# Column tiles: all high weight halves and then all low ones, and a fifth score product of 128 rows

## The chip, the cores and the metric

The kernel runs on one core of a Trainium2 chip. The metric is device time in microseconds (us). The engines are TensorE (PE; its weight loads are listed apart as PEld), VectorE (DVE), ScalarE (ACT), GpSimd (POOL) and SyncE (SP), which here issues the loads.

## The reference

One encoder layer on 256 tokens of width 2048, all in float32:

```
h = RMSNorm(x);  z = h @ w_in  -> q-latent 512 | kv-latent 512 | rotary key 64 | conv 3 x 1024 | memory query 1024 | gates 3 x 2048
A: latent attention, 8 heads, scores = q_nope . k_nope (128 dims) + q_rope . k_rope (64 dims, key shared by the heads)
B: conv_B * dwconv3(conv_C * conv_v)          C: attention of 4 heads into 256 memory tokens
x = x + (sum_i sigmoid(gate_i) * (branch_i @ w_i)) @ w_o
u = dwconv3(RMSNorm(x) @ w_up);  x = x + (silu(a) * b) @ w_down;  out = RMSNorm(x)
```

## The kernel before

Activations stand feature-major, 128 features on the partitions and 256 tokens (T) along the free axis. To keep float32 accuracy each operand is split into two float32r halves: `hi`, a rounded copy that ACT makes (L138 for weights, L195 and L198 for activations), and `lo`, the rest, by a subtraction on DVE (L139, L196 and L199). A split activation chunk is one tile of 512 columns, [hi | lo], 256 each.

Weights come in blocks of 128 x 2048 (1 MB) from the SP queue into three `raw` buffers, and are split into three `hi` and two `lo` buffers. A column tile is 128 output features by 256 tokens. `mm` computes one through `acc`: for each row chunk k the high weights multiply the whole chunk of 512 columns (L165, giving hi.hi in the first PSUM half and hi.lo in the second), then the low weights multiply its high half of 256 columns (L166, lo.hi, summed into the first half). For the last chunk the order is reversed (L162, L163), so that the last matmul closes both halves. `total` adds the two halves (L186 on ACT, L188 on DVE). A tile has 16 row chunks on `h` (the normed inputs of both sub-layers) and on `mg` (the merged branches), 8 on `oa`, `yc` and `om` (the branches' outputs), and 22 on `f` (the feed-forward's inner columns), which come in two blocks of 11, each a call of `acc` of its own.

Elsewhere other helpers do the same: `acc1` (L174 to L176) sums hi.hi, lo.hi and hi.lo into one PSUM half, with 256 columns a matmul; `values` (L371 to L373) has tokens on the partitions and 512 weight columns moving; L521 multiplies the rotary key's weights, halves side by side, by 512 columns.

The stages in order: latents; memory keys and values; rotary key; memory queries and heads; gated convolution with the latent projections and heads in between; gates, branch projections and merge into `mg` (L649 to L653); output projection (L662 on); feed-forward; and the last 512 output columns with tokens on the partitions. Each engine runs its own instructions in order. A planner sets that order ahead of time, by its own simulated time line; so pieces of one job can stand between the matmuls of another.

A head of latent attention (`latent_head`, then `attend`, L437) sums five products into the scores, for each half of the queries: three of split `q_nope` and `k_nope`, then two of the rotary part. A rotary query tile `e` has, for its head, the 64 rows of the high half and the 64 rows of the low half on the two halves of the partitions (which is above which goes by the head's parity); the rotary key `krs` stands there twice, [hi | lo] along the free axis. The fourth product takes all 128 rows of `e` with the key's high half; the fifth takes only the 64 rows of `e`'s high half, with the key's low half.

Of the kernel before, what the change touches and what calls it, by code (L numbers as in the profile page):

```python
# [19 lines left out]
P = 128  # L20
D = 2048
T = 256
# [15 lines left out]

# Columns of the packed per-partition constants.
COLS = {}  # L40
# [10 lines left out]
def _parts(c, bits, n):  # L51
    """c as a sum of n floats of few bits each, so that small integers times them are exact."""
    out = []
    for _ in range(n - 1):
        m, e = math.frexp(c)
        part = math.ldexp(round(math.ldexp(m, bits)), e - bits)
        out.append(part)
        c -= part
    out.append(c)
    return [float(np.float32(x)) for x in out]  # L60
# [16 lines left out]
def tile_kernel(ctx: ExitStack, tc: tile.TileContext, a, out):  # L77
    nc = tc.nc
# [23 lines left out]

# [1 line left out]
    cols = const.tile([P, NCOLS], F32, name="cols")  # L104
# [17 lines left out]

# [1 line left out]
    def load(src, n=WB, pieces=1):  # L124
# [21 lines left out]

    # A column tile's result stands in two parts, [hi.hi + lo.hi | hi.lo], or is summed in place.
    def psum(pool=mmps, tag="mm"):
# [7 lines left out]
    def acc(ps, hi, lo, off, xs, first, final):  # L156
        n = len(xs)
        for k, x in enumerate(xs):
            s = slice(off + k * P, off + (k + 1) * P)
            start, stop = first and k == 0, final and k == n - 1  # L160
            if stop:
                nc.tensor.matmul(ps[:, 0:T], lo[:, s], x[:, 0:T], start=False, stop=False)  # L162
                nc.tensor.matmul(ps, hi[:, s], x, start=start, stop=True)  # L163
            else:
                nc.tensor.matmul(ps, hi[:, s], x, start=start, stop=False)  # L165
                nc.tensor.matmul(ps[:, 0:T], lo[:, s], x[:, 0:T], start=False, stop=False)  # L166

# [15 lines left out]
    def total(ps):  # L183
        """The two parts of a column tile's result, added."""
        hl = temp("hl")
        nc.scalar.activation(hl, ps[:, T:], AF.Copy)  # L186
        t = temp("t")
        nc.vector.tensor_tensor(t, ps[:, 0:T], hl, op=ALU.add)  # L188
        return t

    def split(dst, src, gain=None):
        """src (times a gain) as two float32r halves."""
        w = dst.shape[1] // 2
        if gain is None:
            nc.scalar.activation(dst[:, 0:w], src, AF.Copy)  # L195
            nc.vector.tensor_tensor(dst[:, w:], src, f32(dst[:, 0:w]), op=ALU.subtract)  # L196
        else:
            nc.scalar.activation(dst[:, 0:w], src, AF.Copy, scale=gain)  # L198
            nc.vector.scalar_tensor_tensor(  # L199
                dst[:, w:], src, gain, f32(dst[:, 0:w]), op0=ALU.mult, op1=ALU.subtract  # L200
            )
# [16 lines left out]
    def feature_sums(sq):  # L218
        """Sums over features, tokens on partitions: [128, 2]."""
        ps = atps.tile([P, 2 * T], F32, tag="at", name="psm")  # L220
        for h in range(2):
            nc.tensor.matmul(
                ps[:, h : h + 1], sq[:, h * P : (h + 1) * P], ones[:, 0:1], start=True, stop=True
            )
        return ps[:, 0:2]
# [11 lines left out]
    def spread(r, dst=None):  # L237
        """A factor per token, tokens on partitions, as a row on every partition."""
        ps = atps.tile([P, 2 * T], F32, tag="at", name="pss")
        for h in range(2):  # L240
            dg = tmp.tile([P, P], F32, tag="dg", name="dg")
            nc.vector.tensor_scalar(dg, ident, r[:, h : h + 1], None, op0=ALU.mult)
            nc.tensor.matmul(ps[:, h * P : (h + 1) * P], ones, dg, start=True, stop=True)
        if dst is None:
            return ps[:, 0:T]
        nc.scalar.activation(dst, ps[:, 0:T], AF.Copy)
        return dst

    class Tokens:
        """Feature chunks times the norm's gain, split; and the sums of squares."""  # L250

# [4 lines left out]
        def load(self, n):  # L256
            """The next n chunks, two of them in a tile."""
            i = len(self.raw)
# [17 lines left out]

    # The tensor engine's clock rises while it works, so it starts before the data is there.
    wake = psum(atps, "at")
    for i in range(WAKE):
        nc.tensor.matmul(wake[:, 0:P], ones, ident, start=True, stop=True)  # L280

# [1 line left out]
    tok = Tokens(a["xT"], "mix", "h")  # L283
# [51 lines left out]
    def latent_factor(sq, name, scale):  # L335
        """The token's own norm and the latent's, in one factor."""
        e = tiny.tile([P, 2], F32, tag=name + "e", name=name + "e")
# [7 lines left out]

# [1 line left out]
    kx = []  # L347
# [11 lines left out]
    def values(src, n, nblk, xs, name):  # L359
        """Token-major values, split: for each half of the tokens [hi, lo] of 512 columns."""  # L360
        ps = [psum() for _ in range(2)]
# [26 lines left out]

# [1 line left out]
    pos = half(slot("pos", I32), 0)  # L390
# [21 lines left out]
    def rope(x, w):  # L412
        """x holds halves of 32 partitions; rotated in place, w columns of T."""
        sw = slot("sw")
# [9 lines left out]

# [1 line left out]
    def products(q, k):  # L426
        """The products of split queries and keys, [dims, hi | lo]."""
        return [(q[:, 0:T], k[:, 0:T]), (q[:, T:], k[:, 0:T]), (q[:, 0:T], k[:, T:])]

    def attend(terms, row, vslices, name, res):  # L430
        """terms: queries and keys to multiply, [dims, 256]; row: a factor per key; vslices: the
        split values' [128 keys, 128 dims] by key half. Adds [dims, 256 queries] tiles, split,
        to res."""
        ps = atps.tile([P, 2 * T], F32, tag="at", name="pss")
# [46 lines left out]
    def latent_head(h):  # L481
        r = slice(64 * (h % 2), 64 * (h % 2) + 64)
        e = half(qr[h // 2], h % 2)
        c = slice((h % 4) * P, (h % 4 + 1) * P)
        return attend(
            products(qn[h], kn[h]) + [(e, krs[:, 0:T]), (e[r], krs[r, T:])], half(fb, 0),
            [[(vh[:, c], vl[:, c]) for vh, vl in vn[h // 4]]], f"oa{h}_", oa,
        )
# [13 lines left out]
    def advance(start=None):  # L502
        """A stage of each head under way, then the first of another."""
        for g in list(flying):
            if next(g, 0) == 0:
                flying.remove(g)
        if start is not None:
            next(start)
            flying.append(start)

    # The rotary key, twice over, on partitions 0-63 and 64-127: one column tile holds the
    # halves of its 64 columns, which the sum then brings together.
    raw = next(load(a["wkr"], KC * ROPE))
# [9 lines left out]

# [1 line left out]
    qx = []  # L525
# [16 lines left out]

# [1 line left out]
    def conv(x, dst, w, wi, wn):  # L544
        """Three taps along tokens; w: the name of the taps' columns."""
        nc.scalar.activation(dst, x, AF.Copy, scale=col(w, wn + wi))  # L546
# [40 lines left out]
    def rotary_queries():  # L587
        hi, lo = block(a["wuq"][2])
        for i in range(2):
# [4 lines left out]
            rope(q, 2)  # L594
            # For each head its two halves above each other; the keys stand there twice.
            lows = slot("ql", F32R)
# [33 lines left out]

# [1 line left out]
    mg = [slot(f"mg{i}", F32R) for i in range(KC)]  # L632
# [22 lines left out]

# [1 line left out]
    x2 = [slot(f"xr{i}") for i in range(KC // 2)]  # L657
# [13 lines left out]

# [1 line left out]
    rfb = []  # L673
# [42 lines left out]

    # ---- the last columns with tokens on partitions, so that one half of the tokens is done,
    # normed and stored while the other is still multiplied ----
    gains = slot("gains")
# [85 lines left out]
def _rows(w):  # L805
    """[K, N] in column tiles: [tile, partition, row chunk, 128]."""
    k, n = w.shape
# [3 lines left out]
def _blocks(w, per):  # L811
    """Column tiles, `per` of them in a block: [block, partition, per * rows]."""
    t = _rows(w)
# [4 lines left out]
def _wide(w, per):  # L818
    """[K, N] in pieces of `per` row chunks by 512 columns: [piece, partition, per * 512]."""
    k, n = w.shape  # L820
# [4 lines left out]
def _colmajor(v):  # L825
    """[n * 128] as a column per 128."""
    return np.asarray(v).reshape(-1, P).T
# [83 lines left out]
```

## Time and profile before

| | us |
|---|---|
| median of 3 runs | 1663.72 (1663.1 to 1663.75) |
| span of the profiled execution | 1660.7 |
| PE busy | 1649.4 |
| DVE busy | 1136.8 |
| ACT busy | 843.2 |

The profiled execution gives a span from the first to the last instruction; the runs' time has about 3 us beside it. Matmuls are pipelined, so their busy times overlap, and the distance from start to start is what one costs. A wait of an engine is put down to what ended it.

### The profile page before, as it was taken

The numbers are of one execution on the slowest core, as the hardware profiler recorded it, in microseconds if no ns is written. First come the engines' busy times: TensorE is split into PE (matmuls) and PEld (weight loads), VectorE is DVE, ScalarE is ACT, GpSimd is POOL, SyncE is SP. The second block draws the span as 40 slices with busy tenths as digits, with TensorE's granted clock in tenths as the row PEclk, the third lists the DMA queues.
The fourth block names the chain that finished last, engine by engine and source line by source line (L and its number), as shares of the span: only waits on it lengthen the run. The fifth ranks groups of instructions, "written<-read, shape, count | busy, mean of one in ns | idle before, by whom it ended". The sixth has DMA issues, their size and how long they took to land.

```text
span 1660.7 us, 23629 instructions
## 1 busy us (share of the span) xinstructions
PE 1649.4 (99%) x9626; PEld 1444.8 (87%) x9626; DVE 1136.8 (68%) x1535; ACT 843.2 (51%) x1118; POOL 11.7 (1%) x23
## 2 busy tenths in 40 slices
PE   9999999999999999999999999999999999999998
PEld 9998898888888888888888888888888888888886
DVE  8756787676666666666666777777555777777554
ACT  8644555544545445444454655555444555555552
POOL 0000010000000000000000000000000000000000
PEclk9999999999999999999999999999999999999999
DMA  9555455344555554555565555554556555554563
GB/s 327 208 181 179 170 172 184 142 163 152 180 194 184 181 197 181 183 198 178 190 222 197 185 196 178 186 194 156 178 187 210 192 192 178 191 190 154 187 211 114
DMA packets 52443, 308.97 MB, mean 186 GB/s; under 512 B 6000, under 2 KB 7536, under 8 KB 22256
## 3 DMA queue, kind: packets, MB, share of 16 engines
q1 hardware_dynamic: 50688, 305.82, 52.2%
q8 instruction: 76, 1.25, 0.3%
q10 hardware_dynamic: 1008, 1.12, 0.2%
q0 software_dynamic: 640, 0.52, 0.1%
q14 instruction: 31, 0.25, 0.0%
HBM read 304.17 MB, written 2.10 MB: 184 GB/s over the span
## 4 chain that ended last, share of the span: by engine, by line
PE 98%; DMA 1%; issue 0%; DVE 0%; ACT 0%; SPq 0%; POOLq 0%; POOL 0%; DVEq 0%
PE ps L165 52%; PE ps L166 26%; PE ps L163 4%; PE ps L174 2%; PE ps L175 2%; PE ps L176 2%; PE ps L162 2%; PE pss L437 1%; PE ps L372 1%; PE ps L373 1%; PE ps L371 1%; PE ps L736 0%; PE ps L738 0%; PE ps L737 0%; DMA raw<-in_wkv 0%
## 5 line engine op out<-in xcount | busy, mean ns | idle before, releaser
L139 DVE TENSOR_TENSOR lo<-raw,hi 128x2048 fp32r<-128x2048 f32 (+2 forms) x312 | 649.7, 2083 | 371.5 <-PE ps L162 286.1
L165 PE MATMUL ps<-h,hi 128*128 128x512 f32 x2520 | 898.4, 398 | 0.0
L166 PE MATMUL ps<-h,lo 128*128 128x256 f32 x2520 | 708.3, 281 | 0.0
L138 ACT ACTIVATE hi<-raw 128x2048 fp32r<-128x2048 f32 (+2 forms) x312 | 543.6, 1744 | 81.1 <-PE ps L165 37.1
L165 PEld LDWEIGHTS ps<-h,hi 128*128 128x128 f32 x2520 | 473.4, 188 | 107.7
L166 PEld LDWEIGHTS ps<-h,lo 128*128 128x128 f32 x2520 | 475.8, 189 | 8.1
L186 ACT ACTIVATE hl<-ps 128x256 f32<-128x256 f32 x253 | 97.1, 384 | 440.8 <-PE ps L163 439.4
L165 PE MATMUL ps<-f,hi 128*128 128x512 f32 x588 | 208.7, 398 | 0.0
L166 PE MATMUL ps<-f,lo 128*128 128x256 f32 x588 | 165.4, 281 | 0.1
L165 PEld LDWEIGHTS ps<-f,hi 128*128 128x128 f32 x588 | 110.5, 188 | 25.6
L166 PEld LDWEIGHTS ps<-f,lo 128*128 128x128 f32 x588 | 111.0, 189 | 1.8 <-DVE lo L139 0.4
L188 DVE TENSOR_TENSOR t<-ps,hl 128x256 f32<-128x256 f32 x253 | 105.8, 418 | 9.3 <-ACT hl L186 9.3
L165 PE MATMUL ps<-mg,hi 128*128 128x512 f32 x240 | 85.1, 397 | 0.0
L546 ACT ACTIVATE v<-u,taps 128x256 f32<-128x256 f32 x88 | 44.8, 510 | 70.1 <-DVE u L683 70.1
L547 DVE SCALAR_TENSOR_TENSOR v<-u,taps,v 128x255 f32<-128x255 f32 x88 | 42.5, 484 | 48.8 <-ACT v L546 48.8
L166 PE MATMUL ps<-mg,lo 128*128 128x256 f32 x240 | 67.2, 281 | 0.0
L163 PE MATMUL ps<-h,hi 128*128 128x512 f32 x168 | 67.2, 400 | 0.0
L165 PEld LDWEIGHTS ps<-mg,hi 128*128 128x128 f32 x240 | 45.0, 188 | 10.2
L162 PE MATMUL ps<-h,lo 128*128 128x256 f32 x168 | 47.4, 282 | 0.0
L166 PEld LDWEIGHTS ps<-mg,lo 128*128 128x128 f32 x240 | 45.3, 189 | 0.8
L195 ACT ACTIVATE f<-si 128x256 fp32r<-128x256 f32 x44 | 18.4, 417 | 52.6 <-DVE si L689 52.6
L550 DVE SCALAR_TENSOR_TENSOR v<-u,taps,v 128x255 f32<-128x255 f32 x88 | 42.5, 484 | 3.0
(259 smaller groups left out, 1845.4 us busy)
## 6 DMA issues: line engine op xcount, KB each, us to landing
raw<-in_wup SPq DMA_DIRECT2D x88, 1024.0 KB, 4.8
raw<-in_win SPq DMA_DIRECT2D x83, 1024.0 KB, 4.8
raw<-in_wdn SPq DMA_DIRECT2D x56, 704.0 KB, 4.1
raw<-in_wo SPq DMA_DIRECT2D x16, 1024.0 KB, 4.8
raw<-in_wmk SPq DMA_DIRECT2D x8, 1024.0 KB, 4.9
raw<-in_wmv SPq DMA_DIRECT2D x8, 1024.0 KB, 4.8
raw<-in_woa SPq DMA_DIRECT2D x8, 1024.0 KB, 4.8
raw<-in_woc SPq DMA_DIRECT2D x8, 1024.0 KB, 4.7
```

Of the source, the lines that this page charges most:

```text
L138: nc.scalar.activation(hi[:, s], raw[:, s], AF.Copy)
L139: nc.vector.tensor_tensor(lo[:, s], raw[:, s], f32(hi[:, s]), op=ALU.subtract)
L162: nc.tensor.matmul(ps[:, 0:T], lo[:, s], x[:, 0:T], start=False, stop=False)
L163: nc.tensor.matmul(ps, hi[:, s], x, start=start, stop=True)
L165: nc.tensor.matmul(ps, hi[:, s], x, start=start, stop=False)
L166: nc.tensor.matmul(ps[:, 0:T], lo[:, s], x[:, 0:T], start=False, stop=False)
L174: nc.tensor.matmul(p1, hi[:, s], x[:, 0:T], start=start, stop=False)
L186: nc.scalar.activation(hl, ps[:, T:], AF.Copy)
L188: nc.vector.tensor_tensor(t, ps[:, 0:T], hl, op=ALU.add)
L546: nc.scalar.activation(dst, x, AF.Copy, scale=col(w, wn + wi))
L547: nc.vector.scalar_tensor_tensor(dst[:, 1:T], x[:, 0 : T - 1], col(w, wi), dst[:, 1:T], op0=ALU.mult, op1=ALU.add)
L550: nc.vector.scalar_tensor_tensor(dst[:, 0 : T - 1], x[:, 1:T], col(w, 2 * wn + wi), dst[:, 0 : T - 1], op0=ALU.mult, op1=ALU.add,)
```

## The change

`acc` no longer alternates. A call first issues the high matmuls of its row chunks, then all its low ones; where the call closes the tile, the high matmul of the last chunk is kept back and comes last. For the two blocks of `down` the first call issues 11 highs and 11 lows, the second 10 highs, 11 lows and one high. `latent_head` gives the fifth product all 128 rows of `e` and of the key's low half; this adds the product of the two low halves to the scores. The rest of the diff takes away comments and docstrings.

```
     def acc(ps, hi, lo, off, xs, first, final):
         n = len(xs)
-        for k, x in enumerate(xs):
-            s = slice(off + k * P, off + (k + 1) * P)
-            start, stop = first and k == 0, final and k == n - 1
-            if stop:
-                nc.tensor.matmul(ps[:, 0:T], lo[:, s], x[:, 0:T], start=False, stop=False)
-                nc.tensor.matmul(ps, hi[:, s], x, start=start, stop=True)
-            else:
-                nc.tensor.matmul(ps, hi[:, s], x, start=start, stop=False)
-                nc.tensor.matmul(ps[:, 0:T], lo[:, s], x[:, 0:T], start=False, stop=False)
+        ks = [slice(off + k * P, off + (k + 1) * P) for k in range(n)]
+        whole = n - 1 if final else n
+        for k in range(whole):
+            nc.tensor.matmul(ps, hi[:, ks[k]], xs[k], start=first and k == 0, stop=False)
+        for k in range(n):
+            nc.tensor.matmul(ps[:, 0:T], lo[:, ks[k]], xs[k][:, 0:T], start=False, stop=False)
+        for k in range(whole, n):
+            nc.tensor.matmul(ps, hi[:, ks[k]], xs[k], start=False, stop=True)
...
     def latent_head(h):
-        r = slice(64 * (h % 2), 64 * (h % 2) + 64)
         e = half(qr[h // 2], h % 2)
...
-            products(qn[h], kn[h]) + [(e, krs[:, 0:T]), (e[r], krs[r, T:])], half(fb, 0),
+            products(qn[h], kn[h]) + [(e, krs[:, 0:T]), (e, krs[:, T:])], half(fb, 0),
```

## Rows read from the trace of the kernel before

**Rows 1.** The page's busy times by engine, and the core's span and granted clock.

```profile
PE 1649.4 (99%) x9626; PEld 1444.8 (87%) x9626; DVE 1136.8 (68%) x1535; ACT 843.2 (51%) x1118; POOL 11.7 (1%) x23
...
core 0: 1660.7 us, clock 0.998
```

**Rows 2.** Waits of PE: line, waited for, us in total, times, longest.

```profile
PE pso L755 <- DVE dg L753: 2.7, 1, 2.7
PE ps L280 <- POOL ident masks.py:199: 1.5, 1, 1.5
PE ps L174 <- ACT h L198: 1.1, 1, 1.1
```

**Rows 3.** The chain that ended last, share of the span by line.

```profile
PE ps L165 52%; PE ps L166 26%; PE ps L163 4%; PE ps L174 2%; PE ps L175 2%; PE ps L176 2%; PE ps L162 2%; PE pss L437 1%; PE ps L372 1%; PE ps L373 1%; PE ps L371 1%; PE ps L736 0%; PE ps L738 0%; PE ps L737 0%; DMA raw<-in_wkv 0%
```

**Rows 4.** PE groups: line, names, shapes, count | busy us, mean ns | idle before.

```profile
L165 PE MATMUL ps<-h,hi 128*128 128x512 f32 x2520 | 898.4, 398 | 0.0
...
L165 PE MATMUL ps<-f,hi 128*128 128x512 f32 x588 | 208.7, 398 | 0.0
...
L165 PE MATMUL ps<-mg,hi 128*128 128x512 f32 x240 | 85.1, 397 | 0.0
...
L165 PE MATMUL ps<-yc,hi 128*128 128x512 f32 x112 | 40.2, 398 | 0.0
```

**Rows 5.** Timeline of PE, up projection: start us, us, engine, line, operation.

```profile
1301.41 0.40 PE L165 MATMUL ps<-h,hi 128*128 128x512 f32 x1
1301.64 0.28 PE L166 MATMUL ps<-h,lo 128*128 128x256 f32 x1
...
1305.65 0.40 PE L165 MATMUL ps<-h,hi 128*128 128x512 f32 x1
```

**Rows 6.** Timeline of PE, the rotary key's weights, and the next line.

```profile
145.87 3.79 PE L521 MATMUL ps<-h,wk 128*128 128x512 f32 x16
149.49 0.39 PE L165 MATMUL ps<-h,hi 128*128 128x512 f32 x1
```

**Rows 7.** Timeline of PE in `acc1`: first and last of 25 consecutive starts.

```profile
53.04 0.28 PE L174 MATMUL ps<-h,hi 128*128 128x256 f32 x1
...
55.92 0.28 PE L174 MATMUL ps<-m,hi 128*128 128x256 f32 x1
```

**Rows 8.** Timeline of PE, one latent head's ten score products and what follows.

```profile
276.02 0.52 PE L437 MATMUL pss<-kn,qn 128*128 128x256 f32 x3
276.38 0.60 PE L437 MATMUL pss<-krs,qr 128*128 128x256 f32 x2
276.90 0.62 PE L437 MATMUL pss<-kn,qn 128*128 128x256 f32 x3
277.36 0.59 PE L437 MATMUL pss<-krs,qr 128*128 128x256 f32 x2
277.88 0.50 PE L165 MATMUL ps<-h,hi 128*128 128x512 f32 x1
278.22 0.28 PE L166 MATMUL ps<-h,lo 128*128 128x256 f32 x1
```

**Rows 9.** Busy time by stretch: us, then each engine's busy us (instructions).

```profile
150.00:420.00 270.00, 270.00 (x1654) 238.81 (x1654) 198.55 (x311) 138.63 (x212) 4.26 (x8) 1.00 0.47 165
```

**Rows 10.** The page's group of weight low halves on DVE, with idle before.

```profile
L139 DVE TENSOR_TENSOR lo<-raw,hi 128x2048 fp32r<-128x2048 f32 (+2 forms) x312 | 649.7, 2083 | 371.5 <-PE ps L162 286.1
```

**Rows 11.** Timeline of DVE and PE where the output projection begins.

```profile
814.34 2.29 DVE L139 TENSOR_TENSOR lo<-raw,hi 128x2048 fp32r<-128x2048 f32 x1 [0.77 <-PE ps L162]
816.54 0.42 DVE L196 TENSOR_TENSOR mg<-mg,mg 128x256 fp32r<-128x256 f32 x1
...
818.70 0.42 DVE L196 TENSOR_TENSOR mg<-mg,mg 128x256 fp32r<-128x256 f32 x1 [0.48 <-ACT mg L195]
...
814.37 0.40 PE L165 MATMUL ps<-mg,hi 128*128 128x512 f32 x1
```

**Rows 12.** Group of the low halves' weight loads on PE.

```profile
L166 PEld LDWEIGHTS ps<-h,lo 128*128 128x128 f32 x2520 | 475.8, 189 | 8.1
```

## The prediction

> **What bounds the kernel now.** I read the totals first: TensorE (PE) is busy for 1649.4 of 1660.7 us, VectorE (DVE) for 1136.8 and ScalarE (ACT) for 843.2, at a granted clock of 0.998, the 2.4 GHz level [rows 1]. A busy PE need not be a PE at its best, so the waits come next: its three longest waits on other engines add up to 5.3 us (2.7 at the very end, 1.5 and 1.1 at the start) [rows 2]. The chain of what ended last gives 52% + 26% + 4% + 2% of the span to the four matmul lines of `acc` (L165, L166, L163, L162) [rows 3]. So the end is set by the distance from one matmul's start to the next, above all in the column tiles. A matmul's own duration (398 ns for 512 columns, [rows 4]) says little, for matmuls overlap; starts have to be subtracted.
>
> **Part 1, the order of the column tiles.** It adds and removes no instruction: each column tile has the same high matmuls (512 columns) and low ones (256 columns), and as many weight loads. Only their neighbours change.
>
> How many neighbours change: `acc` issues 2520 high/low pairs on `h`, 588 on `f`, 240 on `mg`, 112 on `yc`, and 112 each on `oa` and `om`, whose rows repeat that of `yc` [rows 4], in all 3684; with them come the reversed last pairs of L162/L163. By the code a tile of 16 row chunks has 15 such pairs, one of 8 has 7, one of 22 (two blocks of 11) has 21: 168 + 16 tiles, 3 x 16 tiles and 28 tiles, 260 together. After the change a tile has one switch from high to low and one back, the 28 tiles with two blocks have two. So of 3684 pairs 260 + 28 keep a switch and 3684 - 288 = **3396** high-low-high alternations become one step in a run of highs and one in a run of lows.
>
> What an alternation costs: in an undisturbed stretch the high matmul at 1301.41 and the one at 1305.65 are 12 pairs apart (the low ones stand between, the first at 1301.64): 4.24 / 12 = 353.3 ns a pair [rows 5].
>
> What the runs cost: before shows both kinds elsewhere. The 16 matmuls of L521 have fresh weights of 128 columns each and 512 moving columns, as the high run will; from the first, at 145.87, to the next line's at 149.49 are 16 steps, 3.62 / 16 = 226.3 ns; the merged row alone gives (3.79 - 0.39) / 15 = 226.7, where 0.39 is a high matmul's duration there [rows 6]. I take 226.7. `acc1` (L174 to L176) multiplies high and low weights by 256 columns into one PSUM half, as the low run will: 53.04 to 55.92 are 24 steps, 2.88 / 24 = 120.0 ns [rows 7]. Together 346.7 ns.
>
> So an alternation made into runs is worth 353.3 - 346.7 = 6.6 ns, and 3396 x 6.6 = **22.4 us**. The bounds: if the remaining switches got cheaper too, 3684 x 6.6 = 24.3; below, zero, if the 353.3 has another cause than the alternation, and half (11.2) if pieces of other work, which the planner places between matmuls, break up the runs. I take 22.4, since both rows of runs have the same shapes, type and clock as the new ones.
>
> [...]
>
> **Part 2, 128 rows for the fifth product.** It is one matmul of 64 rows in each half of each of 8 heads, 16 in all, each last but for the work that follows. One head in starts [rows 8]: three matmuls of 128 rows from 276.02 to 276.38 (0.36, so 0.12 each); then the fourth product and the 64-row one, 0.52 to the next start where two of 0.12 would be 0.24; then three again, which take 0.46 instead of 0.36; then 0.52 again; then a high matmul, 277.88 to 278.22, 0.34 where the high one at 1301.41, after 256 columns too, takes 0.23 [rows 5]. So a 64-row matmul costs about 0.28 before and under it and 0.10 behind it, 0.38 us, over a 128-row one. 16 x 0.38 = **6.1 us**, all on PE, which waits for nobody there; DVE is busy 198.6 of the 270 us of that stretch [rows 9], so nothing else is late next. Added work: 64 more rows in the same 256 columns and 128 weight columns, which the first three products of the head price at 0.12. The rows of `e` that are newly read are those which the fourth product reads already, so no wait is added. Bounds: 0 if the delay came from the fifth product's place and not its rows, 6.1 above.
>
> The Trainium skill's page "TensorE: Matmul & The Clock Gate", section "Why this matters for your kernels", has a matmul of few rows take the same time as one of 128. By that part 2 would be worth nothing. The trace shows 0.52 us where 0.24 would stand.
>
> **What the order moves besides.** Low halves are needed later: the first low matmul of a 16-chunk tile comes 16 x 0.227 - 0.227 = 3.4 us into the tile, not 0.23, so a late `lo` is easier to hide. The last low matmul stays the one before the end, so the two `lo` buffers come free when they did; DVE, which sits idle 371.5 us before L139 and most of it for just that release [rows 10], loses about 22 us of that idleness and keeps the rest. No DMA and no queue entry moves. What is needed earlier is the input chunk: the 15th comes after 14 x 0.2267 = 3.17 us, not 14 x 0.353 = 4.95. That matters only where a stage starts on chunks just made, at the output projection: its first matmul is at 814.37, so chunk 14 is wanted at 817.54, and DVE writes its low half from 816.54 for 0.42, to 816.96; chunk 15 is first wanted by a low matmul at 814.37 + 15 x 0.2267 + 15 x 0.12 = 819.57 and is done at 818.70 + 0.42 = 819.12 [rows 11]. Both hold by 0.4 to 0.6 us. I cost this at nothing; if DVE puts one more weight split of 2.29 us [rows 11] ahead, PE waits up to 1.8 us, and behind PE everything.
>
> **The sum.** 22.4 + 6.1 = 28.5 us off a span of 1660.7: 1632.2. The median of the runs is 1663.7, 3.0 above the span, and nothing outside the span changes: 1663.7 - 28.5 = **1635.2 us**, 1.7% faster.
>
> **Rivals.**
> (a) The order doesn't matter: either the gap of 6.6 ns comes from the surroundings of the column tiles (for it: the two rows of runs lie in the first 150 us; against: those stretches have DVE and ACT at work too), or the planner, which orders each engine by its own estimates, mixes highs and lows again. Then only part 2 stays: 1663.7 - 6.1 = 1657.6. [...]
> (b) The 64 rows don't matter and the place does (the score products begin with key weights that PE hasn't read before): 1663.7 - 22.4 = 1641.3. Against it: the delay comes twice in each head, both times round the 64-row matmul and never round the first three [rows 8]. By the Trainium skill's rule on few rows ("Why this matters for your kernels", above) the time would be this one.
> (c) Slower: a run of lows becomes bound by weight loads. Each low matmul would have to hide a fresh load of 128 columns under 256 columns instead of 512; a load lasts 189 ns [rows 12]. At 189 a low one, a pair costs 226.7 + 189 = 415.7, 62.4 more than now, 3396 x 62.4 = 212 us: 1663.7 + 212 - 6.1 = 1870. It decides from a low step of 120.0 + 6.6 (what a pair gains at 120.0) + 1.8 (part 2's 6.1 us over 3396 pairs) = 128.4 ns on. Against it: `acc1` loads fresh weights at every step at 120.0 [rows 7].
>
> **How the numbers follow.** Forecast 0.80, (a) 0.09, (b) 0.03, (c) 0.05, and 0.03 that new waits eat up what part 2 alone gives. About 0.2% (3.3 us) is what a measurement here can tell from no change. Faster: 0.80 + 0.09 + 0.03 = 0.92; within it 0.03; slower 0.05. The range: below, 24.3 + 6.1 = 30.4 gives 1633.3, and 1 us for the 10 ns to which starts are read, 1632; above, half of part 1 and all of part 2 less 1.8 of waiting, 1663.7 - 11.2 - 6.1 + 1.8 = 1648. It holds the forecast's cases and (b), 0.83.
>
> **What would show it.** In the trace after: high steps of about 227 ns and low steps of 120 inside a tile, a 16-chunk tile of about 5.56 us instead of 5.65; 64-row matmuls gone and a head's ten score matmuls at 0.12 each; no PE wait over 2 us but the one at the end; DVE's idle time before L139 down by some 20 us. Wrong it would be if high steps stayed at 233 to 236 ns within a run, if low steps rose over 128, or if the matmuls still alternate.

## The result, and the profile after

The changed kernel takes 1642.5 us (1642.26 to 1643.4, 4 runs) against 1663.61 of the kernel before (4 runs): a ratio of 0.9874, 95% interval 0.986 to 0.9888, 1.3% faster. The forecast was 1635.2 us and a range from 1632 to 1648. The time lies in the range, but of the 28.5 us that the sum promised 21.1 came, and in the profiled executions 20.2 (span 1660.7 to 1640.5). The question is where the other 7 to 8 went.

Busy times by engine, from the page of the kernel after, beside [rows 1]:

```profile
span 1640.5 us, 23631 instructions
...
PE 1626.7 (99%) x9626; PEld 1447.5 (88%) x9626; DVE 1135.0 (69%) x1535; ACT 840.0 (51%) x1118; POOL 11.6 (1%) x23
```

The same 9626 matmuls and weight loads, 22.7 us less of PE. The chain still lies in the column tiles; the last high matmul of a tile now has line 165, the other highs 161, all lows 163 (after, beside [rows 3]):

```profile
PE ps L161 51%; PE ps L163 29%; PE ps L165 4%; PE ps L173 2%; PE ps L174 2%; PE ps L175 2%; PE ps L371 1%; PE ps L372 1%; PE ps L370 1%; PE pss L436 1%; PE ps L734 0%; PE ps L736 0%; PE ps L735 0%; DMA raw<-in_wkv 0%; PE pst L460 0%
```

The waits of PE after (us in total, times, longest), beside [rows 2]:

```profile
PE pso L753 <- DVE dg L751: 2.7, 1, 2.7
PE ps L161 <- DVE t L187: 2.1, 1, 2.1
PE ps L279 <- POOL ident masks.py:199: 1.5, 1, 1.5
PE ps L173 <- ACT h L197: 1.3, 1, 1.3
PE ps L173 <- DVE cv L560: 0.6, 1, 0.6
```

The second and the last are new: 2.7 us in which PE waits for VectorE, in a kernel whose PE waited for nobody between its first stage and its last.

One column tile of the up projection, from the timeline of PE after (start us, us, then the line, the operation and how many were merged), beside [rows 5]:

```profile
1296.18 0.40 PE L165 MATMUL ps<-h,hi 128*128 128x512 f32 x1
1296.41 3.58 PE L161 MATMUL ps<-h,hi 128*128 128x512 f32 x15
1299.83 2.08 PE L163 MATMUL ps<-h,lo 128*128 128x256 f32 x16
1301.75 0.40 PE L165 MATMUL ps<-h,hi 128*128 128x512 f32 x1
```

The runs are there. From 1299.83 to 1301.75 are 16 low steps: 120.0 ns each, as forecast. From 1296.18 to 1299.83 are 16 high steps, 3.65 / 16 = 228 ns; the forecast was 226.7. The tile is 5.57 us long, forecast 5.56. The same run of highs, asked for from its sixth step on, shows where the difference stands:

```profile
1297.34 2.65 PE L161 MATMUL ps<-h,hi 128*128 128x512 f32 x11
```

The last 11 steps take (1299.83 - 1297.34) / 11 = 226 ns, the first five (1297.34 - 1296.18) / 5 = 232 ns.

One latent head after, beside [rows 8]:

```profile
279.04 0.52 PE L436 MATMUL pss<-kn,qn 128*128 128x256 f32 x3
279.39 0.40 PE L436 MATMUL pss<-krs,qr 128*128 128x256 f32 x2
279.63 0.52 PE L436 MATMUL pss<-kn,qn 128*128 128x256 f32 x3
279.99 0.40 PE L436 MATMUL pss<-krs,qr 128*128 128x256 f32 x2
280.24 1.09 PE L161 MATMUL ps<-h,hi 128*128 128x512 f32 x4
```

Ten score products in 1.20 us, 0.12 each; before they took 1.86.

VectorE's idle time before the weight split, beside [rows 10], went from 371.5 to 346.0 us, 25.5 less, where some 20 were forecast:

```profile
L139 DVE TENSOR_TENSOR lo<-raw,hi 128x2048 fp32r<-128x2048 f32 (+2 forms) x312 | 649.3, 2083 | 346.0 <-PE ps L163 272.1
```

### The profile page after: what moved, and what is told of

Its sections match the earlier page's. It is cut to its first block, busy times and chain, and to the rows that moved or that the text cites. A ratio compares the mean times of both kernels' runs of the same rounds, so it can differ in the third digit from the quotient of the medians.

```text
span 1640.5 us, 23631 instructions
## 1 busy us (share of the span) xinstructions
PE 1626.7 (99%) x9626; PEld 1447.5 (88%) x9626; DVE 1135.0 (69%) x1535; ACT 840.0 (51%) x1118; POOL 11.6 (1%) x23
## 4 chain that ended last, share of the span: by engine, by line
PE 98%; DMA 1%; DVE 1%; issue 0%; ACTq 0%; ACT 0%; SPq 0%; POOLq 0%; POOL 0%; DVEq 0%
PE ps L161 51%; PE ps L163 29%; PE ps L165 4%; PE ps L173 2%; PE ps L174 2%; PE ps L175 2%; PE ps L371 1%; PE ps L372 1%; PE ps L370 1%; PE pss L436 1%; PE ps L734 0%; PE ps L736 0%; PE ps L735 0%; DMA raw<-in_wkv 0%; PE pst L460 0%
## 5 line engine op out<-in xcount | busy, mean ns | idle before, releaser
L139 DVE TENSOR_TENSOR lo<-raw,hi 128x2048 fp32r<-128x2048 f32 (+2 forms) x312 | 649.3, 2083 | 346.0 <-PE ps L163 272.1
L161 PE MATMUL ps<-h,hi 128*128 128x512 f32 x2520 | 606.5, 391 | 2.1 <-DVE t L187 2.1
L163 PEld LDWEIGHTS ps<-h,lo 128*128 128x128 f32 x2688 | 345.0, 191 | 13.0
L163 PE MATMUL ps<-h,lo 128*128 128x256 f32 x2688 | 350.2, 283 | 0.0
L161 PE MATMUL ps<-f,hi 128*128 128x512 f32 x588 | 144.0, 391 | 0.0
L163 PEld LDWEIGHTS ps<-f,lo 128*128 128x128 f32 x616 | 81.4, 191 | 4.4
L163 PE MATMUL ps<-f,lo 128*128 128x256 f32 x616 | 82.8, 282 | 0.0
L165 PE MATMUL ps<-h,hi 128*128 128x512 f32 x168 | 66.6, 396 | 0.0
L161 PE MATMUL ps<-mg,hi 128*128 128x512 f32 x240 | 57.3, 390 | 0.0
L681 DVE TENSOR_TENSOR u<-t,fb 128x256 f32<-128x256 f32 x88 | 37.3, 425 | 2.9
L174 PE MATMUL ps<-m,lo 128*128 128x256 f32 x128 | 35.9, 284 | 0.0
L175 PE MATMUL ps<-m,hi 128*128 128x256 f32 x128 | 35.9, 284 | 0.0
```

The lines of the kernel that those rows point to most:

```text
L139: nc.vector.tensor_tensor(lo[:, s], raw[:, s], f32(hi[:, s]), op=ALU.subtract)
L161: nc.tensor.matmul(ps, hi[:, ks[k]], xs[k], start=first and k == 0, stop=False)
L163: nc.tensor.matmul(ps[:, 0:T], lo[:, ks[k]], xs[k][:, 0:T], start=False, stop=False)
L165: nc.tensor.matmul(ps, hi[:, ks[k]], xs[k], start=False, stop=True)
L174: nc.tensor.matmul(p1, lo[:, s], x[:, 0:T], start=False, stop=False)
L175: nc.tensor.matmul(p1, hi[:, s], x[:, T:], start=False, stop=stop)
```

## The experiments

Each kernel was timed beside the kernel before on the same chip; its time there was 1662.85 us for the first four, 1663.03 for the next four and 1663.71 for the last three.

### Each part by itself

The order alone puts back the fifth product of 64 rows; the rows alone put back the alternating `acc`.

```
 order alone:  products(qn[h], kn[h]) + [(e, krs[:, 0:T]), (e[r], krs[r, T:])]   # new acc
 rows alone:   products(qn[h], kn[h]) + [(e, krs[:, 0:T]), (e, krs[:, T:])]      # old acc
```

> The new order of the column tiles with the old fifth product of 64 rows. If the two parts add up and the 64 rows cost what their rows showed (0.38 us each, 16 of them, 6.1 us), the time is 1642.5 + 6.1 = 1648.6 us. If the place of the fifth product and not its rows made the delay, it stays at 1642.5.

Measured: 1648.23 us, ratio 0.9909 (0.9893 to 0.9926), 14.6 us less than before.

> The old alternating order with the fifth product of 128 rows. If the 64 rows made the delay: 1663.6 - 6.1 = 1657.5 us, and a head's score products at 0.12 us each. If the place made it: 1663.6. If the order's gain and the rows' depend on one another, this and the run with the order alone don't add up to the 21.1 us of the whole change.

Measured: 1656.4 us, ratio 0.9963 (0.995 to 0.9976), 6.45 us less. The sum of the two, 21.1, is the whole change: the parts don't depend on one another, and the 64 rows and not the place made the delay. With the rows alone a head is as short as after the whole change (timeline of PE, the rows alone; the first of the head's two halves and the start of the second):

```profile
276.13 0.52 PE L437 MATMUL pss<-kn,qn 128*128 128x256 f32 x3
276.49 0.40 PE L437 MATMUL pss<-krs,qr 128*128 128x256 f32 x2
276.73 0.52 PE L437 MATMUL pss<-kn,qn 128*128 128x256 f32 x3
```

So the missing 7 us are all missing from part 1: 14.6 instead of 22.4.

### Is it the change of width, or the change between weight buffers?

Alternating as before, but the low matmuls as wide as the high ones:

```
-                nc.tensor.matmul(ps[:, 0:T], lo[:, s], x[:, 0:T], start=False, stop=False)
+                nc.tensor.matmul(ps, lo[:, s], x, start=False, stop=False)
```

> The kernel before, alternating, but its low matmuls multiply all 512 columns, so that high and low weights still alternate and the width no longer does; it adds the product of the two low halves to the second half of each column tile. If the 6.6 ns of an alternation belong to the change of width, all steps are 226.7 ns, a pair 453.4, and the time is 1663.6 + 3684 x 100.1 ns + 260 x 107 ns = 2060 us. If they belong to the change between the two weight buffers, a pair stays 6.6 ns longer, 460 ns: 2084 us.

Measured, one run: 2061.2 us, as the first theory has it, 23 us under the second. The steps (timeline of PE, alternating wide lows; first and last of 14 steps):

```profile
1299.95 0.39 PE L165 MATMUL ps<-h,hi 128*128 128x512 f32 x1
1300.17 0.39 PE L166 MATMUL ps<-h,lo 128*128 128x512 f32 x1
...
1303.12 0.39 PE L165 MATMUL ps<-h,hi 128*128 128x512 f32 x1
```

3.17 / 14 = 226.4 ns, whichever buffer the weights come from: the same as in the run of L521 [rows 6]. What an alternation costs belongs to matmuls of 512 and 256 columns standing beside one another. (With the width goes the part of PSUM that is written, one half or both; no run parts the two.)

### How long must a run be?

Four highs, four lows, and so on, in each tile; its last high still comes last:

```
+        for g in range(0, n, 4):
+            group = range(g, min(g + 4, n))
+            whole = [k for k in group if not (final and k == n - 1)]
+            for k in whole:
+                nc.tensor.matmul(ps, hi[:, ks[k]], xs[k], start=first and k == 0, stop=False)
+            for k in group:
+                nc.tensor.matmul(ps[:, 0:T], lo[:, ks[k]], xs[k][:, 0:T], start=False, stop=False)
```

> As the changed kernel, but four highs, then four lows, and so on. Theory: each run of highs has a start-up of its own; after the change the steps of a run read 233, 236, 228 to 229, 232, 231 and then 227 ns, the lows 114 and then 120. A group of four pairs is then 233 + 236 + 228.6 + 232.2 + 114 + 3 x 120 = 1404 ns, 351.0 a pair, so a tile of 16 chunks is about 5617 ns (5653 before, 5567 after) and of the order's 20.2 us in whole tiles 20.2 x 50 / 86 = 11.7 are lost: 1642.5 + 11.7 = 1654.2 us. Rival, each switch costs the same whatever the run's length: 11 of the 14 removed alternations stay removed, 20.2 x 3 / 14 = 4.3 are lost: 1646.8 us.

Measured: 1647.31 us, ratio 0.9904 (0.989 to 0.9919). By the time alone the rival is right. The trace says that neither is. Between two last highs of tiles (timeline of PE, groups of four):

```profile
1300.35 0.39 PE L167 MATMUL ps<-h,hi 128*128 128x512 f32 x1
1300.58 1.09 PE L163 MATMUL ps<-h,hi 128*128 128x512 f32 x4
1301.51 0.63 PE L165 MATMUL ps<-h,lo 128*128 128x256 f32 x4
1301.98 1.09 PE L163 MATMUL ps<-h,hi 128*128 128x512 f32 x4
...
1305.96 0.40 PE L167 MATMUL ps<-h,hi 128*128 128x512 f32 x1
```

A tile takes 5.61 us (median 5.605); the theory wanted 5.617, the rival 5.585. Whole tiles lose about 0.04 us each of their gain of 0.09, which would be 8.3 us over 260 tiles (37 ns in 184 tiles of 16 chunks, 4 in 48 of 8, 46 in 28 of 22). That the time rose by 4.8 and not by 8.3 has another reason: the two new waits for VectorE, 2.7 us, are not in this kernel, whose three longest waits of PE are 2.7, 1.6 and 1.5 us, at its end and in its beginning. The rival's number came out by that accident.

What a tile of 16 chunks has over 16 x 346.7 = 5547 ns of steady steps is then: alternating 106 ns for 15 rounds (5653 ns; the highs of the last chunk and of the next tile's first stand together), about 7 a round; groups of four 58 ns for four rounds, 14.5 a round; whole runs 20 ns for one round (5567 ns). Few rounds cost less in sum, but each more.

### Can the last round be saved?

Every second tile is turned round, so that the highs of two tiles make one run:

```
+        turns.append(final)
+        if not first:
+            order = [(0, k) for k in range(n)] + [(1, k) for k in range(n)]
+        elif not final or sum(turns) % 2:
+            order = [(1, k) for k in range(n)] + [(0, k) for k in range(n)]
+        else:
+            order = [(1, 0)] + [(0, k) for k in range(n)] + [(1, k) for k in range(1, n)]
```

> The changed kernel with every second column tile turned round (one high, all lows, then the other highs), and the second block of a down tile lows first, so that the highs of neighbouring tiles stand together. Theory: a round from highs to lows and back costs 20 ns over the steady steps when long runs stand on both sides (a tile of 16 is 5566.7 ns where 16 x 346.67 would be 5546.7; one of 22 with two rounds is 7666.7, 40 over) and 6.7 when only one high stands between lows. Two tiles of 16 then have 26.7 instead of 40, a down tile 20 instead of 40: 116 pairs of tiles x 13.3 + 28 x 20 ns = 2.1 us, 1642.5 - 2.1 = 1640.4 us, and up to 2.8 less if the two new waits of PE go as well. Rival: what a tile has over the steady steps belongs to its start and end and not to the switches: 1642.5.

Measured: 1653.1 us, ratio 0.9938 (0.9923 to 0.9953), 10.6 slower than the change. Neither theory has that. The waits of PE tell half of it (the kernel with turns):

```profile
PE ps L171 <- DVE t L212: 4.9, 1, 4.9
PE ps L171 <- DVE t L195: 3.0, 1, 3.0
```

The planner made another order of everything, with 7.9 us of waits round the latent projections, 5.2 more than the 2.7 that the change brought. The clock tells more. The 10 us behind the end of either wait (start and end, us, PE's busy us and instructions, granted clock, share and GB/s of the DMA engines):

```profile
232.78:242.78 10.00, 10.00 (x57) 0.85 0.57 204
269.16:279.16 10.00, 10.00 (x52) 0.79 0.31 107
```

PE had waited 3.0 and 4.9 us, and for part of the time behind that it was granted the 1.2 GHz level; in the change the 10 us behind its wait of 2.1 us have 1.00. An estimate of what the clock cost is 10 x 0.15 + 10 x 0.21 = 3.6 us. Waits and clock are 8.8 of the 9.8 us between the two profiled executions (1650.3 and 1640.5). So the turns were tried again only from the gates on, with the alternating order ahead of them (below).

> The old order up to the gates and the turned tiles from there on. By the sum of the two theories: 1641.0 less 100 pairs of tiles x 13.3 ns and 28 x 20 ns, 1.9 us: 1639.1 us. If the turns bring nothing: 1641.0.

Measured: 1642.49 us, ratio 0.9874 (0.9859 to 0.9889), beside 1641.16 for the same without turns on the same chip. The turns bring nothing. Two tiles (timeline of PE):

```profile
1298.96 2.08 PE L184 MATMUL ps<-h,lo 128*128 128x256 f32 x16
1300.88 0.40 PE L182 MATMUL ps<-h,hi 128*128 128x512 f32 x1
1301.11 2.08 PE L184 MATMUL ps<-h,lo 128*128 128x256 f32 x16
1303.03 7.25 PE L182 MATMUL ps<-h,hi 128*128 128x512 f32 x31
1310.12 2.08 PE L184 MATMUL ps<-h,lo 128*128 128x256 f32 x16
```

From 1298.96 to 1310.12 are 11.16 us, twice 5.57 is 11.14. The lone high takes 0.23 us; the run of 31 behind it has 7.09 / 31 = 228.7 ns a step, 2 over the steady 226.7 although it is twice as long. The same run from its eleventh step on:

```profile
1305.36 4.92 PE L182 MATMUL ps<-h,hi 128*128 128x512 f32 x21
```

These 21 steps take (1310.12 - 1305.36) / 21 = 226.7 ns; the ten ahead of them take (1305.36 - 1303.03) / 10 = 233. The cost of a round isn't paid at the switch alone, but in the first steps of the highs behind it: five after one run of lows (the timeline after, above), ten after two runs of lows with a lone high between them. So "20 ns a round" doesn't carry over to another arrangement, where more steps are long; why the steps behind the lows are long at all is open.

### Whose are the two new waits?

VectorE and PE where the longer one lies, from the timelines of the kernel after (DVE, then PE):

```profile
229.16 2.29 DVE L139 TENSOR_TENSOR lo<-raw,hi 128x2048 fp32r<-128x2048 f32 x1 [1.36 <-PE ps L163]
231.37 0.42 DVE L187 TENSOR_TENSOR t<-ps,hl 128x256 f32<-128x256 f32 x1
...
228.96 0.39 PE L165 MATMUL ps<-h,hi 128*128 128x512 f32 x1
229.19 0.60 PE L460 MATMUL pst<-ident,p 128*128 128x128 f32 x4
231.84 1.42 PE L161 MATMUL ps<-h,hi 128*128 128x512 f32 x5 [2.05 <-DVE t L187]
```

The last high of a column tile starts at 228.96. VectorE is idle, but the tile's last low has just freed a `lo` buffer, so it begins the next weight split, 2.29 us, and sums the tile only behind that, at 231.37; the next tile of PE is placed right behind the transposes and starts when that sum is done, the case that I had named for the output projection. Two kernels tried to take the wait away.

A sixth PSUM bank for column tiles:

```
-    mmps = ctx.enter_context(tc.tile_pool(name="mmps", bufs=5, space=PSUM))
-    atps = ctx.enter_context(tc.tile_pool(name="atps", bufs=3, space=PSUM))
+    mmps = ctx.enter_context(tc.tile_pool(name="mmps", bufs=6, space=PSUM))
+    atps = ctx.enter_context(tc.tile_pool(name="atps", bufs=2, space=PSUM))
```

> The changed kernel with six PSUM banks for column tiles and two for the rest, instead of five and three. The changed kernel has two waits of PE that the kernel before didn't have, 2.1 us at 229.8 and 0.7 at 241.7. Theory: a tile's first matmul waits there for a bank whose sum on VectorE stands behind a weight split of 2.29 us; with a bank more the waits go, and the time is 1642.5 - 2.8 = 1639.7 us, if the two banks that are left don't make new ones. Rival: the wait isn't the bank's; it stays, 1642.5.

Measured: 1652.71 us, ratio 0.9934 (0.9917 to 0.995), slower than the change by 10. PE waits with six banks:

```profile
PE ps L173 <- DVE t L204: 4.4, 1, 4.4
...
PE ps L161 <- DVE qr L591: 2.8, 1, 2.8
PE po L470 <- ACT ph L464: 2.3, 1, 2.3
```

The old waits went and worse ones came, 9.5 us in all. Behind two of them (2.3 and 4.4 us) the granted clock averages 0.84 over 10 us, by the same estimate another 3.2 us. This doesn't tell whether the bank was the cause, since the whole order changed with it.

The old order ahead of the gates, where the list `grouped` is still empty and `acc` runs the loop of before:

```
+        if not grouped:
+            for k, x in enumerate(xs):
...
+            return
...
     mg = [slot(f"mg{i}", F32R) for i in range(KC)]
+    grouped.append(True)
```

> The changed kernel with the old alternating order up to the gates, that is in the memory queries and the gated convolution, and the new order from there on. Theory: the new order gains little in that stretch (the order alone: 0.47 us between the first head and the branch projections, 0.99 in the memory queries, less 3.1 lost to new waits round the latent projections), so with the old order there the new waits go and the time is 1642.5 - 1.5 = 1641.0 us. Rival: the waits are independent of the order (run to run), and the 32 tiles there gain 86 ns each: 1642.5 + 2.8 = 1645.3.

Measured: 1641.16 us, ratio 0.9866 (0.9852 to 0.9881). It was timed a second time, beside the changed kernel:

> The changed kernel once more, beside the two below on the same chip: 1642.5 us, and its two waits of PE, 2.1 and 0.6 us, at the same places.

> The old order up to the gates, the new one from there, once more beside the changed kernel: 1641.1 us if the 1.4 us between the two were not the chip's; equal to the changed kernel if they were.

Measured: the change 1642.82 us, ratio 0.9876 (0.986 to 0.9893), with its waits of 2.1 and 0.6 us at their places; the old order up to the gates 1641.29, ratio 0.9864 (0.985 to 0.9879). On one chip the second is 1.5 us quicker, as expected, though the intervals overlap. Its three longest waits of PE:

```profile
PE pso L767 <- DVE dg L765: 2.7, 1, 2.7
PE ps L292 <- POOL ident masks.py:199: 1.5, 1, 1.5
PE ps L186 <- ACT h L210: 1.3, 1, 1.3
```

So the waits belong to the order that the planner made for the stretch from the memory queries to the last head, and they come with the new `acc` there: with the order alone they are there too, with the rows alone not.

### A version that beats both

`acc1` takes three steps of 120 ns for a chunk [rows 7]; a chunk in the new order takes 346.7. The memory keys and the query latents stand ahead of the difficult stretch and don't need the single PSUM half, so they get the new `acc` (`grouped` is filled from the start, emptied behind the memory keys and filled again at the gates):

```
-        latent(mm1(*wblock(2 if i == 0 else 1), 0, xs), zq[i], qsq, "qn", i)
+        latent(total(mm(*wblock(2 if i == 0 else 1), 0, xs)), zq[i], qsq, "qn", i)
...
-        pend.append(mm1(*block(a["wmk"][i]), 0, ms))
+        pend.append(total(mm(*block(a["wmk"][i]), 0, ms)))
```

> As the one above, and the memory keys and the query latents (12 tiles of 16 chunks) computed like the other column tiles, highs of 512 columns and then lows of 256, instead of three products of 256 columns. Their steps are 16 x 360 = 5760 ns a tile now; a whole tile of the new order is 5567: 12 x 193 ns = 2.3 us less, 1638.8 us, if the sums of the two halves that come with it (0.4 us each on ScalarE and VectorE) hide and the memory's chunks are there in time, which are wanted 1.8 us earlier. If chunk or sum comes late, PE waits and the gain is lost: 1641.1.

Measured: 1638.82 us, ratio 0.9851 (0.9837 to 0.9866); beside it on the same chip 1641.29 without this step and 1642.82 for the change. A tile of the memory keys (timeline of PE) is 87.78 - 82.21 = 5.57 us long:

```profile
82.21 0.40 PE L178 MATMUL ps<-m,hi 128*128 128x512 f32 x1
82.44 3.58 PE L174 MATMUL ps<-m,hi 128*128 128x512 f32 x15
85.86 2.08 PE L176 MATMUL ps<-m,lo 128*128 128x256 f32 x16
87.78 0.40 PE L178 MATMUL ps<-m,hi 128*128 128x512 f32 x1
```

## Why the prediction was right, and where a term was too large

**What bounds the kernel** held: PE busy time and span fell together, and VectorE gave up idle time, not work.

**Part 2** held in mechanism and size: 6.1 us forecast, 6.45 measured by itself. The rival that place and not rows made the delay fell with the rows alone. The Trainium skill's "TensorE: Matmul & The Clock Gate", section "Why this matters for your kernels", from which the rival's time followed, has a matmul of few rows take the same time as one of 128. The trace doesn't agree for one 64-row matmul among 128-row ones, and no run here has 64-row matmuls among their like. The Trainium skill's "TensorEngine Tiling (Array Packing)", section "Key Properties", says that changing the tiling mode drains the engine. The trace agrees as far as it goes: the delay stood on the steps into and out of the 64-row matmul, 0.52 us for two where 0.24 is usual, and 0.10 behind it [rows 8]. That this delay is such a drain is not shown.

**Part 1** held in mechanism and was too large by a third: 22.4 us forecast, 14.6 measured with the order alone, and 20.2 - 6.1 = 14.1 in the profiled executions. The rival that the order doesn't matter fell: the same matmuls take 353 ns a pair alternating and 347 in runs. The Trainium skill's "TensorE: Matmul & The Clock Gate", section "Back-to-back issue gap", gives N / 2.4 + 2.5 ns as the gap of an isolated matmul. That is 215.8 and 109.2 ns by an estimate for these widths; the steps in runs here, 226.7 and 120.0, are 11 over it. Low steps in runs stayed at 120.0, so the third rival, lows bound by weight loads, fell too. The step that failed is the sum "3396 x 6.6 = 22.4", which I took over its own lower bounds: it lets every step of a run be a steady one and costs the remaining rounds and the waits at nothing more than before. What stands in the place of the missing 8.3 us of the profiled execution:

- The switches that remain are dearer. I left them at 6.6 ns a round; a round between long runs is 20. A tile of 16 chunks gains 86 ns and not 14 x 6.6 = 92, one of 8 (2.820 to 2.793 us) 27 and not 40, one of 22 (7.773 to 7.667) 106 and not 125: 184 x 6 + 48 x 13 + 28 x 19 ns, 2.3 us.
- The new waits, 2.7 us. I had the mechanism, a weight split of 2.29 us ahead of what PE needs, and its price, but looked for it at the output projection alone. There it didn't come: 32 highs of several tiles follow one another from 805.45, the first low comes at 812.72, and the last low half of `mg` was written at 809.78 + 0.42 = 810.20. It came where the tiles have short other work between them. The forecast's sign "no PE wait over 2 us but the one at the end" was missed by this, with 2.1 us.
- The tiles of the attention stretch, whose runs are cut by transposes and score products. From the first memory query to the first branch projection the order alone takes 271.1 us (150.24 to 421.37), before 269.5 (149.49 to 418.96). Without the 2.6 us of its new waits it saves 0.9 there, where 32 whole tiles would save 32 x 86 ns = 2.8. This is the "runs broken up" of my lower bound: 1.9 us.
- 0.8 us stood in the first stage, where the memory keys began at 54.16 instead of 53.40. The order of PE, VectorE and ScalarE there is the same in both kernels, and other runs have 53.5 and 55.0; the kernel with the old order up to the gates has 54.63 in its first run and 53.45 in its second. So this goes by the run and not by the change. After, the larger part of it follows a wait of ScalarE for a weight load, 1.41 us up to 23.45.
- The 0.6 us that are left are spread over the other stages and were not traced further.

**What I would change**: 6.6 ns was a difference between two steady states, and a run reaches its own only at the sixth step; the first two read 233 and 236 ns, which I had named as a sign of being wrong if a whole run kept them. The rows to look at were the starts of runs, and I had taken averages over runs alone.

## What to carry to other kernels

Matmuls of one width belong together: on a PE that never waits, sorting 512- and 256-column matmuls into runs of 16 gave 86 ns a tile of 5.65 us, and runs of four only about half of it. Keep the row count of matmuls equal in a sequence: one 64-row matmul among 128-row ones cost 0.38 us, three of its kind. And where a planner makes the order, an edit in one place moves work elsewhere: compare PE's waits by line before and after, look at the granted clock behind them, and if new ones stand in one stretch, leave that stretch as it was.

## What the runs showed of the hardware

- Alternating 512 and 256 columns costs 6.6 ns a pair over the steady steps of either width (353.3 against 226.7 + 120.0); alternating weight buffers at equal width costs nothing (226.4 ns a step over 14 steps). The cause wasn't found.
- The cost of a change from 256 to 512 columns falls on the first steps of the wide run: five of 232 ns on average behind 16 narrow matmuls, ten of 233 behind 16 narrow, one wide and 16 narrow; the steps after them take 226.7.
- A step of 512 columns is 226.7 ns and one of 256 is 120.0, at the granted 2.4 GHz level, with a fresh weight load each. The 256 columns between them cost 106.7 ns, so about 13 ns of either step don't go with its columns, and one wide matmul beats two narrow ones by 13 ns (0.2267 us against 0.240), which is what the fastest version uses.
- Behind waits of PE of 2.3 to 4.9 us the granted clock averaged 0.79 to 0.85 over 10 us in the kernels with turns and with six banks, part of that time at the 1.2 GHz level; behind waits of 2.1 us (the change) and 2.8 us (six banks) it stayed at 1.00.
